# Eight experts on one core: x of the first two experts loaded into 64 rows instead of 128, b1 on another queue, the first weight load cut in two

## The chip, the core and the metric

The kernel runs on one core of a Trainium2 chip. The metric is the device time of one execution in microseconds (us); the time shown is the median of several executions. A core has TensorE (PE; its weight loads are listed apart as PEld), VectorE (DVE), ScalarE (ACT), GpSimd (POOL) and SyncE (SP). Sixteen DMA engines move data between the device memory (HBM) and the on-chip memory (SBUF, 128 rows called partitions). Programs hand transfers to them from SP, ACT or POOL.

## What is computed

Eight experts, each a two-layer network over its own 256 tokens: 512 inputs, 2048 hidden units, 512 outputs, all tensors fp32 in memory.

```python
h = np.matmul(x, w1) + b1[:, np.newaxis, :]     # x (8, 256, 512), w1 (8, 512, 2048)
h = np.maximum(h, 0)
return (np.matmul(h, w2) + b2[:, np.newaxis, :]).astype(np.float32)   # w2 (8, 2048, 512)
```

The weights are 8 x 2 x 4 MB = 67.1 MB of fp32, x and the output 4.2 MB each. Every weight is used once per token block, so the whole of it has to come in once.

## The kernel before

**Data.** w1 and w2 of an expert are loaded by POOL (`load_w1`, L82; `load_w2`, L88) and turned from fp32 into fp16 on the way, so 4 MB are read and 2 MB written, 16 KB in each of the 128 rows. POOL's transfers stand in one queue (q0 in the profile) in the order in which they are issued. x of experts 2 and 3, and of 4 to 7, comes the same way (`load_x`, L72). x of experts 0 and 1 is different: SP loads it as fp32 (L190), each expert as 128 rows of 4 KB (two tokens to a row), into two buffers of the output's pool, and DVE casts it (L201). SP's and ACT's transfers stand in queues of their own (q1 and q10).

**Stages.** `first_product(e)` (L114) makes the hidden layer of an expert: 16 column blocks `j`, each of 4 matmuls (L121) into one of three PSUM tiles, which ACT then takes through bias and Relu into `hT` (L128). It needs x transposed (`xT`), which `transposes(e)` (L95) makes on DVE in blocks of 32x32; for expert 0 it is called at the start, for expert e+1 in the middle of `first_product(e)`. A call issues 16 instructions of 256 elements a row where an x row holds two tokens (L109) or four (L112), and 8 of 512 elements where a row holds eight (L112; experts 4 to 7 before the change). `second_product(e)` (L166) runs three stages later (LAG = 3): bias b2 as a matmul with a row of ones (L171), 32 matmuls (L178), and the results through DVE and ACT (L156, L157) to the output. Results of experts 0 to 3 and 4 to 5 are held and written together by `flush` (L138) behind all weights in POOL's queue; those of 6 and 7 leave at once by SP and ACT (L164).

**Order.** PE's and POOL's instructions keep the order of the program (`ordered`); on DVE and ACT a scheduler decides. The list `ring` (L215 to L225) says in which stage each load is issued. w1 and w2 have three buffers each, so a load waits until the product that used its buffer three experts earlier is over. At the start POOL issues w1 of expert 0 (L84), b2 (L192), b1 (L196), w1 of expert 1, x of experts 2 and 3 (L76) and w1 of expert 2, before its first wait.

**b1.** b1 comes as 32 rows of 2 KB (`b_rows`) and DVE transposes it with four instructions into `b1T` (L208), which the first Relu needs.

Of the kernel before, what the change touches and what calls it, by code (L numbers as in the profile page):

```python
# [10 lines left out]
def kernel(  # L11
# [9 lines left out]
    nc = tc.nc  # L21
    fp32 = mybir.dt.float32
    fp16 = mybir.dt.float16
    E, T, H = x.shape
    M = w1.shape[2]
    P = 128
    nTB = T // P
    nKC = H // P
    nJ = M // P
    B = 32  # L30
    nB = P // B
# [9 lines left out]
    nXF32 = 2  # L41
    X_LOADS = {2: 2, 4: 4}

    def ordered(ins):
        return tc.keep_in_program_order(ins)
# [3 lines left out]
    w2_pool = ctx.enter_context(tc.tile_pool(name="w2", bufs=3))  # L49
    x_pool = ctx.enter_context(tc.tile_pool(name="xp", bufs=1))  # L50
# [3 lines left out]
    out_pool = ctx.enter_context(tc.tile_pool(name="outp", bufs=2))  # L54
# [5 lines left out]
    b1_rows = singles.tile([E * nB, M // nB], fp32)  # L60
    b1T = singles.tile([P, nJ * B + nB - 1], fp32)

    x16 = [None] * E
    xT = [None] * E
    w1_sb = [None] * E
# [15 lines left out]

    def load_w1(e):  # L82
        w1_sb[e] = w1_pool.tile([P, nKC, M], fp16, tag="w1", name="w1sb")
        ordered(nc.gpsimd.dma_start(  # L84
            out=w1_sb[e], in_=w1[e].rearrange("(p kc) m -> p kc m", kc=nKC)
        ))

    def load_w2(e):  # L88
        src = w2[e].rearrange("(p j) h -> p j h", j=nJ)
# [5 lines left out]
    def transposes(e):  # L95


        t, p0, R = x16[e]
        n = R // nTB
        xT[e] = xT_pool.tile([P, nKC, T], fp16, tag="xT", name="xT")  # L100
        for g in range(T // R // B):
            src = t[p0 + B * g : p0 + B * (g + 1)]
            for b in range(nB):
                block = src[:, :, b * (H // nB) : (b + 1) * (H // nB)].rearrange(
                    "p (n tb) (i kc) -> p tb kc n i", tb=nTB, kc=nKC)
                out = xT[e][b * B : (b + 1) * B].rearrange(
                    "p kc (tb g i n) -> p tb g kc n i", tb=nTB, i=B, n=n)
                if n == 1:
                    nc.vector.transpose(out=out[:, :, g, :, 0, :], in_=block[:, :, :, 0, :])  # L109
                    continue  # L110
                for tb in range(nTB):
                    nc.vector.transpose(out=out[:, tb, g], in_=block[:, tb])  # L112
# [71 lines left out]
                    ))  # L184
        store(e, po)

    x32 = []
    for e in range(nXF32):
        x32.append(out_pool.tile([P, nTB, H], fp32, tag="out", name="x32"))
        nc.sync.dma_start(out=x32[e], in_=x[e].rearrange("(p tb) h -> p tb h", tb=nTB))  # L190
    load_w1(0)
    ordered(nc.gpsimd.dma_start(  # L192
        out=b2_sb,
        in_=b2.rearrange("e h -> (e h)").rearrange("(o f) -> o f", o=1),
    ))
    ordered(nc.gpsimd.dma_start(out=b1_rows, in_=b1.rearrange("e (b i) -> (e b) i", b=nB)))  # L196
    nc.vector.memset(ones1, 1.0)  # L197

    for e in range(nXF32):
        t = x_pool.tile([P, nTB, H], fp16, tag=f"x{e}", name=f"x{e}")  # L200
        nc.vector.tensor_copy(out=t, in_=x32[e])  # L201
        x16[e] = (t, 0, nTB)
        if e == 0:
            transposes(e)


    for b in range(nB):
        nc.vector.transpose(  # L208
            out=b1T[b * B : (b + 1) * B, nB - 1 - b : nB - 1 - b + nJ * B],
            in_=b1_rows.rearrange("r (i j) -> r j i", j=nJ),  # L210
# [5 lines left out]
    for s in range(1, E + LAG - 1):  # L216
        if s < E:
            if s in X_LOADS:
                ring.append((s - 2, load_x, (s, X_LOADS[s])))
            ring.append((s - 2, load_w1, (s,)))  # L220
        if s >= LAG:
            ring.append((s - 2, load_w2, (s - LAG,)))
# [43 lines left out]
```

## Time and profile before

| | |
|---|---|
| median of 3 runs | 181.69 us (181.45 to 182.16) |
| profiled execution, first to last instruction (span) | 179.7 us |
| PE busy / DVE busy / ACT busy | 129.1 / 88.0 / 70.2 us |
| read from HBM / written to HBM | 71.39 MB / 4.19 MB |
| DMA queue of POOL (q0) | 38.35 MB, 96.6% of the 16 engines' span |
| DMA queue of SP (q1) / of ACT (q10) | 1.70 MB, 2.4% / 0.39 MB, 0.5% |

The times of runs are device times of a whole execution; the profile knows the span of the profiled one, and no other total of it. The span is 2.0 us below the median, and that difference lies outside the first and last instruction. A queue's megabytes are bytes written (a cast load reads twice as many). A queue's share is the time of its packets over 16 engines times the span; packets on one engine may overlap a little, so sums near or above 100% mean that the engines never stop.

### The profile page before, as it was taken

What the parts mean: (1) busy time and instruction counts of PE and PEld (TensorE: products, weight loads), DVE (VectorE), ACT (ScalarE), POOL (GpSimd) and SP (SyncE); (2) the same over time, 40 slices, a digit from 0 to 9 for tenths busy, and PEclk for the clock granted to TensorE, in tenths of its full rate; (3) what the DMA queues carried; (4) which work ended last, traced back from release to release, by engine and by line L of the source; (5) the groups of instructions that cost most, each with busy time, mean ns of one, the idle gap of its engine ahead of it and who ended that gap; (6) DMA issues with size and microseconds to landing.
All of it is one profiled execution on the core that took longest, in us unless ns stands there. A gap on an engine that the chain in (4) does not pass through costs nothing.

```text
span 179.7 us, 1958 instructions
## 1 busy us (share of the span) xinstructions
PE 129.1 (72%) x784; PEld 85.8 (48%) x784; DVE 88.0 (49%) x125; ACT 70.2 (39%) x151; POOL 13.1 (7%) x28
## 2 busy tenths in 40 slices
PE   0005099969595970899969597969497887999950
PEld 0004079969592320795369244844195332433420
DVE  0999942987000199999999998003200020301010
ACT  0000459969593022483099005950586020020010
POOL 7000002120201010001010001000200021010000
PEclk9999999999998798589999889999999996999996
DMA  5999999999999999999999999999999999999996
GB/s 216 251 226 199 233 212 197 233 224 193 228 230 192 221 233 215 197 230 230 204 208 230 219 193 233 226 193 222 230 215 197 233 206 204 223 212 215 335 420 250
DMA packets 3829, 40.56 MB, mean 226 GB/s; under 512 B 461, under 2 KB 477, under 8 KB 1133
## 3 DMA queue, kind: packets, MB, share of 16 engines
q0 software_dynamic: 3232, 38.35, 96.6%
q1 hardware_dynamic: 476, 1.70, 2.4%
q10 hardware_dynamic: 112, 0.39, 0.5%
q8 instruction: 6, 0.10, 0.2%
q14 instruction: 3, 0.02, 0.0%
HBM read 71.39 MB, written 4.19 MB: 421 GB/s over the span
## 4 chain that ended last, share of the span: by engine, by line
DMA 66%; PE 26%; POOL 2%; another core or an unknown queue 1%; issue 1%; ACT 0%; POOLq 0%
DMA w1sb<-in_w_dram 44%; DMA w2sb<-in_w_dram 22%; PE po L178 18%; PE ph L121 8%; PE po L171 1%; POOL w1sb L84 1%; ACT out L157 0%; POOL x L76 0%; POOL b_sb L192 0%; POOL b_rows L196 0%; POOLq L250 0%
## 5 line engine op out<-in xcount | busy, mean ns | idle before, releaser
L121 PE MATMUL ph<-xT,w1sb 128*128 128x256 f16 x512 | 63.6, 289 | 34.8 <-DMA w1sb<-in_w_dram 23.9
L121 PEld LDWEIGHTS <-w1sb 128*128 128x128 f16 x512 | 59.0, 147 | 40.3 <-DMA w1sb<-in_w_dram 32.6
L178 PE MATMUL po<-w2sb,hT 128*128 128x512 f16 x256 | 61.4, 402 | 9.4 <-DMA w2sb<-in_w_dram 9.4
L112 DVE STREAM_TRANSPOSE xT<-x 32x256 f16<-32x256 f16 (+1 forms) x64 | 53.1, 889 | 25.6 <-DMA x<-in_x_dram 18.7
L128 ACT ACTIVATE hT<-ph,b1T 128x256 f16<-128x256 f32 x128 | 56.2, 474 | 13.6 <-PE ph L121 13.4
L178 PEld LDWEIGHTS <-hT 128*128 128x128 f16 x256 | 25.9, 102 | 44.7 <-issue 19.3
L156 DVE COPY out<-po 32x512 f32<-32x512 f32 (+2 forms) x22 | 15.1, 688 | 54.0 <-PE po L178 53.8
L157 ACT COPY out<-po 32x512 f32<-32x512 f32 (+2 forms) x22 | 12.7, 579 | 69.7 <-PE po L178 69.5
L109 DVE STREAM_TRANSPOSE xT<-x 32x256 f16<-32x256 f16 x32 | 14.0, 436 | 0.5
L93 POOL DMA_DIRECT2D w2sb<-in_w_dram x10 | 5.3, 534 | 72.8 <-PE po L178 72.8
L128 ACT ACT_TABLE_LOAD x1 | 1.3, 1283 | 20.5 <-DVE b1T L208 20.5
L84 POOL DMA_DIRECT2D w1sb<-in_w_dram x8 | 4.5, 558 | 63.2 <-PE ph L121 62.4
L171 PE MATMUL po<-b_sb,ones 1*128 1x512 f16 x16 | 4.8, 379 | 0.0
L208 DVE STREAM_TRANSPOSE b1T<-b_rows 32x512 f32<-32x512 f32 x4 | 4.1, 1035 | 0.1
L201 DVE CAST x<-x 128x1024 f16<-128x1024 f32 x2 | 1.5, 757 | 3.3 <-DMA x<-in_x_dram 3.3
L140 POOL DMA_DIRECT2D out_dram<-out x2 | 1.1, 542 | 10.9 <-ACT out L157 10.9
L171 PEld LDWEIGHTS <-ones 1*128 1x128 f16 x16 | 0.9, 92 | 2.1 <-issue 2.1
L76 POOL DMA_DIRECT2D x<-in_x_dram x2 | 1.1, 552 | 0.0
L197 DVE MEMSET ones<- 1x128 f16 x1 | 0.2, 165 | 0.8 <-PEq L250 0.8
L196 POOL DMA_DIRECT2D b_rows<-in_b_dram x1 | 0.5, 515 | 0.0
L192 POOL DMA_DIRECT2D b_sb<-in_b_dram x1 | 0.5, 513 | 0.0
L250 POOL MEMSET const-float32-0.0<- 128x1 f32 x1 | 0.1, 99 | 0.2 <-issue 0.2
(3 smaller groups left out, 0.3 us busy)
## 6 DMA issues: line engine op xcount, KB each, us to landing
w1sb<-in_w_dram POOLq DMA_DIRECT2D x8, 2048.0 KB, 34.5
w2sb<-in_w_dram POOLq DMA_DIRECT2D x6, 2048.0 KB, 46.8
w2sb<-in_w_dram POOLq DMA_DIRECT2D x4, 1024.0 KB, 24.0
out_dram<-out POOLq DMA_DIRECT2D x1, 2048.0 KB, 26.8
x<-in_x_dram SPq DMA_DIRECT2D x2, 512.0 KB, 3.9
x<-in_x_dram POOLq DMA_DIRECT2D x1, 1024.0 KB, 30.8
out_dram<-out POOLq DMA_DIRECT2D x1, 1024.0 KB, 17.8
x<-in_x_dram POOLq DMA_DIRECT2D x1, 512.0 KB, 24.0
```

Source lines behind the costliest of these rows:

```text
L84: ordered(nc.gpsimd.dma_start(out=w1_sb[e], in_=w1[e].rearrange("(p kc) m -> p kc m", kc=nKC)))
L93: ordered(nc.gpsimd.dma_start(out=w2_sb[e][:, lo : lo + half], in_=src[:, lo : lo + half]))
L109: nc.vector.transpose(out=out[:, :, g, :, 0, :], in_=block[:, :, :, 0, :])
L112: nc.vector.transpose(out=out[:, tb, g], in_=block[:, tb])
L121: ordered(nc.tensor.matmul(out=ph, lhsT=w1_sb[e][:, kc, :].rearrange("p (q j) -> p q j", j=nJ)[:, :, j], rhs=xT[e][:, kc, :], start=(kc == 0),
L128: nc.scalar.activation(out=hT[e][:, j, :].rearrange("p (tb k i) -> p tb k i", tb=nTB, k=split), in_=ph.rearrange("p (tb i k) -> p tb k i", ...
L156: nc.vector.tensor_copy(out=out_sb[at : at + rows, k * nTB, :], in_=po[0][part])
L157: nc.scalar.copy(out=out_sb[at : at + rows, k * nTB + 1, :], in_=po[1][part])
L171: ordered(nc.tensor.matmul(out=t, lhsT=ones1, rhs=b2_sb[0:1, e * H : (e + 1) * H], start=True, stop=False,))
L178: ordered(nc.tensor.matmul(out=po[tb], lhsT=hT[e][:, j, tb * P : (tb + 1) * P], rhs=w2_sb[e][:, j, :], start=False, stop=(j == nJ - 1),))
L201: nc.vector.tensor_copy(out=t, in_=x32[e])
L208: nc.vector.transpose(out=b1T[b * B : (b + 1) * B, nB - 1 - b : nB - 1 - b + nJ * B], in_=b1_rows.rearrange("r (i j) -> r j i", j=nJ),)
```

## The change

x of experts 0 and 1 is loaded by SP as 32 rows of 16 KB for each expert (eight tokens to a row): expert 0 into rows 0 to 31, expert 1 into rows 32 to 63 of one tile. The tile is taken from w2's pool, where it fills one of three buffers. Its cast to fp16 goes into one tile `x01` and is divided: for expert 0 half on DVE and half on ACT, for expert 1 all on ACT. With eight tokens to a row, `transposes` takes the form of 8 instructions of 512 elements for both experts. The b1 load moves from POOL's queue to ACT's, as ACT's first instruction. The first w1 load becomes two transfers, rows 0 to 31 and rows 32 to 127; expert 0's matmuls wait for both. On DVE the four transposes of b1 now stand first, ahead of expert 0's cast and transposes; ACT's table load and two copies of x stand ahead of the first Relu.

```diff
     def load_w1(e):
         w1_sb[e] = w1_pool.tile([P, nKC, M], fp16, tag="w1", name="w1sb")
-        ordered(nc.gpsimd.dma_start(
-            out=w1_sb[e], in_=w1[e].rearrange("(p kc) m -> p kc m", kc=nKC)
-        ))
+        src = w1[e].rearrange("(p kc) m -> p kc m", kc=nKC)
+        rows = P // 4 if e == 0 else P
+        for lo in ((0, rows) if e == 0 else (0,)):
+            hi = rows if e == 0 and lo == 0 else P
+            ordered(nc.gpsimd.dma_start(out=w1_sb[e][lo:hi], in_=src[lo:hi]))
...
-    x32 = []
+    RX = T // B
+    x32 = w2_pool.tile([nXF32 * B, RX, H], fp32, tag="w2", name="x32")
     for e in range(nXF32):
-        x32.append(out_pool.tile([P, nTB, H], fp32, tag="out", name="x32"))
-        nc.sync.dma_start(out=x32[e], in_=x[e].rearrange("(p tb) h -> p tb h", tb=nTB))
+        nc.sync.dma_start(out=x32[e * B : (e + 1) * B], in_=x[e].rearrange("(p r) h -> p r h", r=RX))
+    nc.scalar.dma_start(out=b1_rows, in_=b1.rearrange("e (b i) -> (e b) i", b=nB))
     load_w1(0)
...
-    ordered(nc.gpsimd.dma_start(out=b1_rows, in_=b1.rearrange("e (b i) -> (e b) i", b=nB)))
     nc.vector.memset(ones1, 1.0)
 
+    x01 = x_pool.tile([nXF32 * B, RX, H], fp16, tag="x01", name="x01")
     for e in range(nXF32):
-        t = x_pool.tile([P, nTB, H], fp16, tag=f"x{e}", name=f"x{e}")
-        nc.vector.tensor_copy(out=t, in_=x32[e])
-        x16[e] = (t, 0, nTB)
+        rows = slice(e * B, (e + 1) * B)
+        cut = RX // 2 if e == 0 else 0
+        if cut:
+            nc.vector.tensor_copy(out=x01[rows, :cut], in_=x32[rows, :cut])
+        nc.scalar.copy(out=x01[rows, cut:], in_=x32[rows, cut:])
+        x16[e] = (x01, e * B, RX)
         if e == 0:
             transposes(e)
```

## The prediction, made before the changed kernel was run

> **What bounds the kernel.** I read the DMA lines of the page first, because section 2 shows them full in all slices but the first and last.
>
> ```profile
> DMA  5999999999999999999999999999999999999996
> ...
> q0 software_dynamic: 3232, 38.35, 96.6%
> q1 hardware_dynamic: 476, 1.70, 2.4%
> q10 hardware_dynamic: 112, 0.39, 0.5%
> ```
>
> The three shares add up to 99.5% of the span on all 16 engines. The chain of waits says the same in order of time: loads, then a short piece of PE work that lets the next load be issued, then loads.
>
> ```profile
> 4.00 34.57 DMA w1sb<-in_w_dram
> ...
> 46.12 45.24 DMA w1sb<-in_w_dram
> ...
> 110.12 39.38 DMA w2sb<-in_w_dram
> 149.50 0.04 issue
> 149.54 8.66 PE po L178 x32
> ```
>
> After 149.5 the chain runs on PE, which looks like a PE-bound tail. The busy time by windows corrects that (columns: window, length, busy time and count for PE, PEld, DVE, ACT, POOL, then granted clock, DMA share, GB/s):
>
> ```profile
> 0.00:1.70 1.70, 0.00 (x0) 0.00 (x0) 0.17 (x1) 0.00 (x0) 0.66 (x5) 1.00 0.00 0
> 1.70:2.30 0.60, 0.00 (x0) 0.00 (x0) 0.00 (x0) 0.00 (x0) 0.60 (x2) 1.00 0.49 137
> 2.30:4.50 2.20, 0.00 (x0) 0.00 (x0) 0.24 (x1) 0.00 (x0) 2.20 (x5) 1.00 1.03 408
> ...
> 140.00:166.00 26.00, 23.91 (x102) 9.80 (x100) 3.44 (x5) 2.54 (x5) 2.13 (x4) 0.93 1.01 212
> ...
> 168.20:178.40 10.20, 5.09 (x24) 2.12 (x22) 0.69 (x1) 0.59 (x1) 0.00 (x0) 0.92 0.94 395
> 178.40:179.70 1.30, 0.00 (x0) 0.00 (x0) 0.00 (x0) 0.00 (x0) 0.00 (x0) 0.50 0.00 0
> ```
>
> The engines start at 1.7, stop at 178.4, and have a share near 1 in between, in the tail too, where the held results fill what PE leaves open. So the span is 1.7 us before the first packet, the engines' total work, and 1.3 us after it. Only what changes that work, its start or its gaps counts; PE, DVE and ACT count only where they make a transfer late.
>
> **The change, part by part.** First the x loads, the one part that alters the engines' work. The DMA view of two windows, 0 to 5 us and 5 to 14 us:
>
> ```profile
> q1 hardware_dynamic: 287, 1.05, 54.7%
> ```
>
> ```profile
> q0 software_dynamic: 113, 1.85, 96.6%
> ```
>
> x takes 0.547 x 5.0 = 2.73 us of all 16 engines, in 256 packets of 4 KB: 2.73 x 16 / 256 = 0.171 us each. On each engine POOL's first weight packet begins within some 10 ns of the end of x there (packet records, 4.59 to 5.12 us), so the two queues together leave no hole; a change in x's time moves every later packet by the same amount. After the change x is 64 packets of 16 KB, four to an engine, all into rows 0 to 63. No row of the trace shows that, so I bound it.
>
> Low end: the held results leave in 16 KB packets of 0.611 us (packet records, 168 to 173 us), so x would cost 64 x 0.611 / 16 = 2.44 us, 0.29 us less than now. High end: the 16 KB packets that go into SBUF take 0.966 x 9.0 x 16 / 113 = 1.23 us (second fence), so x would cost 64 x 1.23 / 16 = 4.92 us, 2.19 us more. I take the high end: it is the row with the same size and the same direction, and nothing in this trace shows 16 engines filling 64 rows or fewer at full rate for longer than b1's 64 KB. Against it: those packets read 32 KB each for the cast, which plain x does not, and b1's own 32 rows came at 0.172 us per 4 KB, beside 0.159 for x's commonest packet. So both ends stay in the range.
>
> [...]
>
> The w1 load in two: the same 128 packets of 16 KB in all, one more completion packet on each engine (0.022 us in the packet records). POOL issues one w1 piece more and b1 no longer, so w1 of expert 1 is still issued near 2.9 and of expert 2 near 4.0 us (an issue took 0.5 to 0.67 us). Nobody waits: the first w1 load keeps the engines busy until 14.4. The fp16 pieces arrive at half the byte rate of plain loads, so I add nothing for rows 0 to 31 being filled alone. Cost bounds from no gain to 0.02 us; if the short first piece let weights run beside x while the engines ramp up (share 0.49 in the window 1.70 to 2.30), the gain is at most 0.51 x 0.6 = 0.3 us. I take 0.
>
> b1 on ACT: the same 64 KB, 0.17 us on each engine in either queue, so 0. ACT's issue costs it some 0.4 us (0.38 for its store at L164) before 1.3 us of table load, and nothing is queued behind these two that could run earlier.
>
> Copies of x on ACT: 512 fp32 elements took 0.58 us (L157), so 2048 and 4096 cost at most 2.3 and 4.6 us. Behind them stand the Relus, which wait for PE anyway. With x landed by about 7.1 they end before 14.5; PE has nothing for ACT before that. Cost 0.
>
> DVE, the part that gets heavier:
>
> ```profile
> L112 DVE STREAM_TRANSPOSE xT<-x 32x512 f16<-32x512 f16 x32 | 40.2, 1331 | 19.2 <-DMA x<-in_x_dram 18.7 <-PE ph L121 0.3
> ...
> L109 DVE STREAM_TRANSPOSE xT<-x 32x256 f16<-32x256 f16 x32 | 14.0, 436 | 0.5
> ```
>
> An expert's transposes go from 16 x 0.436 = 7.0 us to 8 x 1.331 = 10.6 us, the same form that experts 4 to 7 use. b1 now stands ahead. It comes behind x on the engines, so it lands near 7.3 us; four transposes of 1.035 us (L208) end at 11.4, the half cast of 2048 elements (twice 0.757) at 12.9, xT of expert 0 at 23.5 us. Before, PE had 12 matmuls done and stood still from 18.05 to 22.28, because ACT waited for b1T. From 22.28 on it needed 8.2 us to the end of the product (POOL's next w1 issue at 30.46). Now: 23.5 + 2.8 (the 12 matmuls) + 8.2 = 34.5 us. POOL's w1 load of expert 3 waits for that. The engines have work until w1 of expert 2 is in, 36.8 us by the first engines before and about 39.0 with x longer: 4.5 us of cover, 2.3 without the longer x (then b1 and the product are 2 us earlier as well). Expert 1's xT is ready at 34.1, in time; its product ends near 41.5 and expert 2's starts then, 0.8 us behind its weights, and waits again for expert 3's weights (47.66 before). So the heavier DVE work is hidden. If the cover were gone, each further microsecond would cost one.
>
> The tile in w2's pool: w2 of expert 2 now waits for the release of x32, over before 15 us; it was issued at 46.65. Cost 0.
>
> Sum: 2.19 us on the span, 179.7 to 181.9; the 2.0 us around it stay, so the median goes from 181.69 to **183.9 us** (+1.2%).
>
> **The rivals.** *The rows do not matter* (no change). x's packets cost 0.153 to 0.171 us per 4 KB wherever they land: between -0.29 and 0, so 181.4 to 181.7 us. For it: b1's 32 rows at 0.172, and 96 rows stored by ACT at 0.159 without any spread; against it: the first lasted under a microsecond, the second reads SBUF and alternates with other packets. A change that did not do what it says (16 KB rows cut again into 4 KB packets) would end here too.
>
> *The start is filled* (faster). Weights in the short first piece run beside x from its first packet: 0.29 from cheaper packets and 0.3 from the ramp give 181.1 us. It decides only if more than 0.91 us comes together, which is 0.3 us more than the rows hold; that could come from the last engine, since w1 of expert 2 landed on 15 engines by 37.14 and on the last at 38.57. I know no reason why x in new rows should cure that.
>
> *The DVE order starves POOL* (slower). If xT of expert 0 comes later than 23.5 by more than the 4.5 us of cover, for example because b1 lands behind much of w1, the queue runs dry; b1 landing at 14 would give 23.5 + 6.7 = 30.2, 2.2 us over the cover, so 183.9 + 2.2 = 186.1 us.
>
> **How the numbers follow.** About 0.5%, 0.91 us, is what a measurement of this kernel can tell from no change. Rows matter, with all or half of the high end: 0.68, its own range 183.0 to 184.4. Rows do not matter: 0.22. Start filled past 0.91 us: 0.06. POOL starved: 0.04. Slower 0.68 + 0.04 = 0.72, same 0.22, faster 0.06. The range reaches from 181.1, which takes in the second case with its gain, to 184.4; it leaves out the last two and the edges.
>
> **What would show it.** Right: q1's 64 packets of 16 KB near 1.2 us each, POOL's first weight packet near 6.9 us instead of 4.6, w1 of expert 0 landing near 17.4 instead of 15.2, every later landing 2 us late, and DMA shares near 1 throughout. Wrong: x packets near 0.61 us, or a DMA share well below 1 between 30 and 45 us (then DVE starved the queue).

## The result and the profile after

The changed kernel takes **183.78 us** (median of 4 runs, 183.63 to 183.88); the kernel before, on the same chip, 181.62 us (181.45 to 182.16). The ratio is 1.011, with a 95% interval of 1.0095 to 1.0125. Forecast were 183.9 us and a range of 181.1 to 184.4. The span grew from 179.7 to 182.0 us, 2.3 us, so the whole difference lies between the first and the last instruction.

The page's DMA lines show queues as full as before, and SP's queue with 284 packets instead of 476, yet 3.4% of the engines' time instead of 2.4%:

```profile
DMA  6999999999999999999999999999999999999995
...
q0 software_dynamic: 3216, 38.28, 95.2%
q1 hardware_dynamic: 284, 1.70, 3.4%
q10 hardware_dynamic: 160, 0.46, 0.7%
```

The bytes in q1 are the same 1.70 MB. One percent more of 182 us is 1.8 us: x has become dear. Its part alone, in the DMA view of 0 to 9 us (packets, MB, share of 16 engines):

```profile
q1 hardware_dynamic: 96, 1.05, 51.2%
q0 software_dynamic: 32, 0.52, 29.1%
q10 hardware_dynamic: 48, 0.07, 3.6%
```

That is 0.512 x 9.0 = 4.61 us for x, where it was 2.73, and 0.036 x 9.0 = 0.32 us for b1. In the packet records the 64 packets of x take 1.273 us in the median, the first of each engine 0.63 to 1.10, the rest up to 1.30. POOL's first weight packet of an engine starts at 7.02 us on average, at 4.77 before: 2.25 us later. From there on, up to 166 us, the engines stay as full as before (columns as in the prediction; a row counts a packet's whole time where the packet starts, so a short window can show more than 1):

```profile
1.70:2.30 0.60, 0.00 (x0) 0.00 (x0) 0.00 (x0) 0.60 (x1) 0.60 (x2) 1.00 1.10 328
2.30:6.70 4.40, 0.00 (x0) 0.00 (x0) 0.60 (x1) 1.08 (x2) 2.23 (x5) 1.00 0.98 212
6.70:30.00 23.30, 8.57 (x60) 7.77 (x61) 23.00 (x20) 10.62 (x16) 0.00 (x0) 1.00 1.02 213
30.00:38.00 8.00, 6.89 (x64) 6.68 (x63) 7.87 (x18) 6.73 (x16) 1.59 (x3) 1.00 1.07 229
38.00:46.00 8.00, 6.78 (x63) 6.55 (x62) 6.51 (x17) 6.60 (x16) 1.06 (x2) 1.00 1.00 213
46.00:166.00 120.00, 96.18 (x562) 60.88 (x561) 53.75 (x52) 48.53 (x105) 6.89 (x13) 0.91 1.02 216
```

The second row is the loss in one line: the engines are as busy as before (0.98), but move 212 GB/s, in a stretch where x moved at 408 before (window 2.30 to 4.50). The fence has no hole between 30 and 46 us (shares 1.07 and 1.00), where a late DVE leaves one in the run with 12.4 us more below (0.26).

The chain of waits now begins differently, on DVE:

```profile
0.73 5.34 DMA b_rows<-in_b_dram
...
29.76 0.51 issue
30.27 1.34 DVE xT L114
31.61 0.14 issue
31.74 7.20 PE ph L123 x64
...
47.65 45.71 DMA w1sb<-in_w_dram
```

Read alone, it would blame b1 and the transposes, 16% of the span between them. It does not know that the loads which PE's work releases at 39 us join a queue that is still full (share 1.00 from 38 to 46 us); two experiments below show that this stretch costs nothing.

### The profile page after: what moved, and what is told of

Read it like the earlier page. It is cut to its first block, busy times and chain, and to the rows that moved or that the text cites. A ratio compares the mean times of both kernels' runs of the same rounds, so it can differ in the third digit from the quotient of the medians.

```text
span 182.0 us, 1945 instructions
## 1 busy us (share of the span) xinstructions
PE 128.2 (70%) x784; PEld 85.8 (47%) x784; DVE 93.3 (51%) x108; ACT 75.8 (42%) x153; POOL 13.0 (7%) x28
## 4 chain that ended last, share of the span: by engine, by line
DMA 50%; PE 26%; DVE 14%; issue 5%; another core or an unknown queue 1%; POOL 1%; ACT 0%; DVEq 0%; POOLq 0%
DMA w1sb<-in_w_dram 25%; DMA w2sb<-in_w_dram 22%; PE po L180 17%; DVE xT L114 11%; PE ph L123 8%; DMA b_rows<-in_b_dram 3%; DVE b1T L214 2%; PE po L173 1%; DVE x L206 1%; ACT out L159 0%; POOL w1sb L88 0%; POOL w2sb L95 0%; DVEq L114 0%; POOLq L95 0%
## 5 line engine op out<-in xcount | busy, mean ns | idle before, releaser
L114 DVE STREAM_TRANSPOSE xT<-x 32x512 f16<-32x512 f16 (+1 forms) x80 | 72.7, 977 | 21.1 <-DMA x<-in_x_dram 19.0
L180 PE MATMUL po<-w2sb,hT 128*128 128x512 f16 x256 | 59.9, 395 | 8.0 <-DMA w2sb<-in_w_dram 8.0
L207 ACT CAST x<-x 32x2048 f16<-32x2048 f32 (+1 forms) x2 | 5.5, 2750 | 4.0 <-DMA x<-in_x_dram 4.0
L206 DVE CAST x<-x 32x2048 f16<-32x2048 f32 x1 | 1.2, 1214 | 0.0
```

What stands on the lines that cost most here:

```text
L180: ordered(nc.tensor.matmul(out=po[tb], lhsT=hT[e][:, j, tb * P : (tb + 1) * P], rhs=w2_sb[e][:, j, :], start=False, stop=(j == nJ - 1),))
L206: nc.vector.tensor_copy(out=x01[rows, :cut], in_=x32[rows, :cut])
L207: nc.scalar.copy(out=x01[rows, cut:], in_=x32[rows, cut:])
```

## The experiments

Theory: the place of x, rows 0 to 63, makes its packets slow (1.273 us in the median) and so keeps the DMA engines busy longer, and the rest follows one for one; the expectations call it the theory of place. Rivals: packet size, the other parts of the change, the DVE order.

**x as before, the rest kept.**

```diff
-    x32 = w2_pool.tile([nXF32 * B, RX, H], fp32, tag="w2", name="x32")
+    x32.append(out_pool.tile([P, nTB, H], fp32, tag="out", name="x32"))      # for e in 0, 1
-        nc.sync.dma_start(out=x32[e * B : (e + 1) * B], in_=x[e].rearrange("(p r) h -> p r h", r=RX))
+        nc.sync.dma_start(out=x32[e], in_=x[e].rearrange("(p tb) h -> p tb h", tb=nTB))
...
```

> The changed kernel with x of experts 0 and 1 loaded and cast as before (128 rows of 4 KB); b1 on ACT's queue and the first w1 load in two stay. Theory (the x load alone costs the time): x's packets 0.16 us again, POOL's first weight packet near 4.8 us, 181.3 to 181.9 us. Rival (the split of w1 or b1 beside x costs part of it): 182.5 us or more.

Measured: 181.77 us, 1.0005 times the kernel before (0.9996 to 1.0014). x took 2.79 us of the engines. The first weight packet of an engine came at 5.22 us on average, not near 4.8: b1's packets, 0.41 us in this run, now stand ahead of it instead of behind it. Without x in 64 rows there is no loss to measure.

**x alone.** The kernel before with the changed load, cast and transposes of x, b1 and w1 as they were.

> The kernel before with x of experts 0 and 1 as 32 rows of 16 KB each, and nothing else of the change. Theory (the x load alone costs the time): x's packets near 1.27 us, first weight packet near 7.0 us, 183.4 to 184.2 us. Rival (the other parts cost): under 182.6 us.

Measured: 183.25 us, 1.0083 (1.007 to 1.0097), a little below the range expected; packets 1.274 us, first weight packet at 6.70 us on average. x makes 1.6 of the 2.2 us by itself. In the DMA view of 0 to 9 us its packets take 53.4%, 4.81 us, which is 2.07 more than before: the time follows the packets here only to about 0.4 us. The 0.5 us missing appear only with the other parts beside it, and two experiments further down look for them.

**The same packets, other rows.** One transfer of 64 rows of 16 KB into rows 32 to 95, 0 to 63, or 64 to 127:

```diff
-    x32 = w2_pool.tile([nXF32 * B, RX, H], fp32, tag="w2", name="x32")
-    for e in range(nXF32):
-        nc.sync.dma_start(out=x32[e * B : (e + 1) * B], in_=x[e].rearrange("(p r) h -> p r h", r=RX))
+    AT = 32        # 0 and 64 in the other two
+    x32 = w2_pool.tile([P, RX, H], fp32, tag="w2", name="x32")
+    nc.sync.dma_start(out=x32[AT : AT + nXF32 * B], in_=x[0:nXF32].rearrange("e (p r) h -> (e p) r h", r=RX))
...                # the casts use the same rows of x01
```

Rows 32 to 95:

> The changed kernel with x of both experts in one transfer of 64 rows of 16 KB into rows 32 to 95 instead of 0 to 63; same packets, same DVE work. [...] Rival of size (a 16 KB packet, or fewer rows than 128, is slow in itself): packets 1.27 us, 183.4 to 184.0 us.

Rows 0 to 63:

> As the kernel with rows 32 to 95, but the one transfer of 64 rows goes into rows 0 to 63. Theory of place: packets 1.2 to 1.3 us, 183.4 to 184.2 us. Rival (two transfers of 32 rows one after the other were the trouble, and one of 64 cures it): packets 0.61 us, near 181.4 us.

Rows 64 to 127:

> As the kernel with one transfer of 64 rows, into rows 64 to 127. [...] Rival (the low rows alone are crowded, by something else that lives or writes there): packets 0.61 us, 181.7 to 182.1 us.

Measured:

| rows | time, us | ratio to before | packet of x, median |
|---|---|---|---|
| 32 to 95 | 181.96 | 1.0015 (1.0006 to 1.0024) | 0.618 us |
| 0 to 63 | 183.66 | 1.0104 (1.0089 to 1.0120) | 1.287 us |
| 64 to 127 | 183.32 | 1.0088 (1.0069 to 1.0107) | 1.280 us |

In the DMA view of 0 to 9 us, rows 32 to 95 first, then rows 0 to 63, then rows 64 to 127:

```profile
q1 hardware_dynamic: 80, 1.05, 31.8%
```

```profile
q1 hardware_dynamic: 80, 1.05, 51.1%
```

```profile
q1 hardware_dynamic: 80, 1.05, 52.6%
```

Packets, bytes, instructions on DVE and their order are the same in the three; the engines' time for x is 2.86, 4.60 and 4.73 us. Only the place of the rows differs. That excludes size and number of rows as the cause of the slow packets, and the third excludes that the low rows alone are crowded: either half is slow (1.287 and 1.280 us), and half of each is fast (0.618). What lies behind this is not shown. The first gains nothing over the kernel before: even with 16 KB packets of 0.618 us x costs 2.86 us, where it was 2.73, because the first packet of an engine takes up to 1.58 us and starts at 2.10 us at the earliest, behind b1 (1.74 us in the changed kernel).

**Packets of 4 KB into the same rows.** Each expert's x in four transfers of 4 KB to a row.

```diff
-        nc.sync.dma_start(out=x32[e * B : (e + 1) * B], in_=x[e].rearrange("(p r) h -> p r h", r=RX))
+        src = x[e].rearrange("(p r) h -> p r h", r=RX)
+        for r in range(0, RX, 2):
+            nc.sync.dma_start(out=x32[e * B : (e + 1) * B, r : r + 2], in_=src[:, r : r + 2])
```

> The changed kernel with each expert's 32 rows of 16 KB fetched in four transfers of 4 KB to a row, into the same rows 0 to 63. Theory of place: 4 KB packets near 0.32 us instead of 0.16, x 4.6 to 5.0 us of the engines, 183.6 to 184.2 us. Rival of size (16 KB packets are slow): packets 0.16 us, 181.6 to 182.0 us.

Measured: 184.26 us, 1.0137 (1.0119 to 1.0156). The time fits the theory, most of the packets do not: their median is 0.172 us. SP needed 5.0 us to issue the eight transfers, POOL's weights began at 2.97 us, and x came in single packets between them until 24 us. Why most were short is not shown. In a stretch where many of x's packets ran together, 2.75 to 3.03 us, 12 of 15 took 0.27 to 0.34 us, the doubled time that the theory asks for. The first weight packets took 1.24 to 2.08 us. Expert 0's x was late as well, and w1 of expert 3 was issued only at 36.23 us. This run mixes several effects. Of its 2.7 us, 1.35 are longer packet times of all queues together; the rest, engines that stand idle in the first 8 us and at the end, stays open.

**Half the amount.** Expert 0's x in 32 rows, expert 1's in 128.

```diff
+    x32 = w2_pool.tile([B, RX, H], fp32, tag="w2", name="x32")
+    nc.sync.dma_start(out=x32, in_=x[0].rearrange("(p r) h -> p r h", r=RX))
+    x32b = out_pool.tile([P, nTB, H], fp32, tag="out", name="x32b")
+    nc.sync.dma_start(out=x32b, in_=x[1].rearrange("(p tb) h -> p tb h", tb=nTB))
...
```

> The changed kernel with expert 0's x alone in 32 rows of 16 KB; expert 1's comes in 128 rows of 4 KB. Theory of place: expert 0's packets 1.2 us, expert 1's 0.16, half the loss: 182.5 to 183.0 us. Rival (a fixed cost of this form of load, whatever its amount): 183.6 us or more, or 181.8 or less.

Measured: 182.62 us, 1.0049 (1.0032 to 1.0066): 1.05 us over the 181.57 of the kernel before, half of the whole change's 2.16. Expert 0's packets took 1.06 us in the median (1.2 expected), expert 1's 0.169.

**DVE's order.** The four transposes of b1 two times and four times, ahead of (or among) expert 0's transposes:

```diff
-    for b in range(nB):
+    for b in [b for _ in range(2) for b in range(nB)]:        # 4 in the second
         nc.vector.transpose(out=b1T[...], in_=...)
```

> The changed kernel with the four transposes of b1 done twice, 4.1 us more on DVE ahead of expert 0's x. Theory (DVE's heavier start is hidden by loads already issued): POOL issues w1 of expert 3 near 35 us instead of 30.9, before the engines run out near 38.9; 183.6 to 184.0 us, no change from the changed kernel. Rival (DVE's order is part of the loss): 185 us or more.

> The changed kernel with the transposes of b1 done four times, 12.4 us more on DVE. Theory: the cover is gone; w1 of expert 3 is issued near 43.3 us, the engines stand idle from 38.9 to some 44.5 us, and the end comes later by that, 188.5 to 190.5 us. Rival (DVE's start never matters): 183.8 us.

Measured: 183.66 us with 4.1 us more, as the changed kernel (183.78). With 12.4 us more the runs spread from 187.5 to 190.3 us, median 189.63, and why they spread is open. The profiled execution, 190.32 us, is the slowest of them, and the ratio, 1.0389 (1.0324 to 1.0454), leaves it out. POOL issued w1 of expert 3 at 35.04 and 42.99 us (30.93 in the changed kernel). The windows of 30 to 46 us, first with 4.1, then with 12.4 us more:

```profile
30.00:38.00 8.00, 6.84 (x63) 6.63 (x62) 7.91 (x11) 6.68 (x16) 1.59 (x3) 1.00 1.06 227
38.00:46.00 8.00, 8.00 (x76) 8.00 (x75) 7.05 (x19) 8.00 (x19) 1.06 (x2) 1.00 0.99 212
```

```profile
30.00:38.00 8.00, 6.28 (x29) 4.78 (x29) 7.86 (x8) 2.63 (x6) 0.00 (x0) 1.00 1.07 229
38.00:46.00 8.00, 6.54 (x54) 6.03 (x52) 7.91 (x10) 5.65 (x13) 1.59 (x3) 1.00 0.26 33
```

The DMA share falls to 0.26 only in the last row: 0.74 x 8 = 5.9 us without transfers. By the packet records the engines run dry between 38.6 and 39.2 us, and the next packets begin at 44.25. The median grew by 5.85 us, the span of the profiled execution by 6.5. So the changed kernel's DVE work lies wholly under loads already issued, with more than 4.1 us to spare.

**The other two parts, beside x in rows 0 to 63.** First the w1 load whole again, then b1 back on POOL's queue:

```diff
-        for lo in ((0, rows) if e == 0 else (0,)):
-            ...
+        ordered(nc.gpsimd.dma_start(out=w1_sb[e], in_=w1[e].rearrange("(p kc) m -> p kc m", kc=nKC)))
```

> The changed kernel with the first w1 load whole again; x in rows 0 to 63 and b1 on ACT's queue stay. The kernel with x alone took 183.25 us, the whole change 183.78 us. If the first piece of w1 (its packets 1.28 and 1.33 us instead of 1.23, all into rows 0 to 31) makes up part of those 0.5 us: first two weight packets of an engine at 1.23 us, 183.5 to 183.7 us. Rival (the split costs nothing, b1 all): 183.8 us.

```diff
-    nc.scalar.dma_start(out=b1_rows, in_=b1.rearrange("e (b i) -> (e b) i", b=nB))
+    ordered(nc.gpsimd.dma_start(out=b1_rows, in_=b1.rearrange("e (b i) -> (e b) i", b=nB)))   # behind b2
```

> The changed kernel with b1 back on POOL's queue behind b2; x in rows 0 to 63 and w1 in two stay. If b1 beside x makes up part of the 0.5 us (its packets took 0.32 us of the engines there, 0.17 on POOL's queue): 183.4 to 183.6 us. Rival (the split of w1 is all): 183.8 us.

Measured: 183.53 (183.45 to 183.62) and 183.50 us (183.47 to 183.61), each about 0.25 below the changed kernel's 183.78 (183.63 to 183.88). Together that is about the 0.5 us that x alone left open. But by their ratios to the kernel before, 1.0101 (1.0085 to 1.0116) and 1.0101 (1.0086 to 1.0116), neither can be told from the changed kernel's 1.011 (1.0095 to 1.0125), so what each part costs is not shown. Without the split an engine's first two weight packets take 1.29 and 1.23 us, with it 1.29 and 1.33.

**A version with what is good in the change.** x of both experts in one transfer of 128 rows of 8 KB, b1 on ACT's queue, w1 whole; DVE casts expert 0's half, ACT expert 1's.

```diff
+    RX = nXF32 * T // P
+    x32 = w2_pool.tile([P, RX, H], fp32, tag="w2", name="x32")
+    nc.sync.dma_start(out=x32, in_=x[0:nXF32].rearrange("e (p r) h -> (e p) r h", r=RX))
...
```

> A version meant to keep what is good: x of both experts in one transfer of 128 rows of 8 KB, cast half on DVE and half on ACT, b1 on ACT's queue, the first w1 load whole. Theory (the engines' total work sets the time): x 2.5 to 2.7 us of the engines, 181.4 to 181.9 us, no measurable gain although ACT no longer waits for b1. Rival (the wait for b1T at the start costs time): 180.7 us or less.

Measured: 181.75 us, 1.0007 (0.9998 to 1.0017). It issues w1 of expert 3 at 26.35 us instead of 30.46, four microseconds earlier, and gains nothing. No version here beats the kernel before.

## Why the prediction was right, step by step

**The bound.** That only the engines' work, start and gaps count was right, in both directions: PE's stall for b1T removed (x as before; 128 rows of 8 KB) bought nothing, and 4.1 us more on DVE cost nothing. The packet times of all queues, added up over the profile and divided by 16 engines, are 179.3 us before. They are 2.0 us more with the change, 2.1 and 1.9 with one transfer into rows 0 to 63 and 64 to 127, 1.8 with x alone, 1.0 with half the amount, and no more with rows 32 to 95; the times grew by 2.16, 2.04, 1.75, 1.63, 1.05 and 0.34 us. So one for one holds to about 0.35 us. The run with 4 KB packets is the exception (1.35 and 2.7).

**The x load.** The step chosen between two bounds, 1.23 us for a 16 KB packet rather than 0.61, was right: 1.273 in the median. The reason given with it, the same size and direction as the weights' packets, was not: into rows 32 to 95 packets of this size and direction took 0.618 us, and only the place of the rows differs there. That the place matters was shown by no row of the trace before; the three placements show it. Here x was in flight from 1.74 to 7.36 us, 187 GB/s by 1.05 MB over 5.6 us. The measured size of the term was 4.61 us, not 4.92, because the first packet of each engine took only 0.63 to 1.10 us: +1.88 instead of +2.19.

**Two terms priced at nothing** were not quite nothing. In the changed kernel's packet records b1 took 0.32 us of the engines instead of 0.17, and an engine's second weight packet 1.33 us instead of 1.23. With x's 1.88 this makes 2.13 of the 2.16 us. The runs that take back one part came out 0.25 us (the split) and 0.28 us (b1) faster, which is not clear of noise, and the packets do not explain it: with b1 back on POOL's queue x's packets took 4.87 us instead of 4.61, so x and b1 together took no less. The price of each part stays open, somewhere between 0.1 and 0.3 us. With x in 128 rows the two together were within the measurement, although b1 took 0.41 us there. That 183.9 came so near to 183.78 is in part luck: x was put 0.31 us too high, and these two terms about as much too low.

**DVE.** The direction was right, the size was not: xT of expert 0 was ready at 21.43 us, not 23.5. b1 landed at 6.07, not 7.3, since its packets went between those of x (2.81 to 4.79 us, x until 7.36) instead of behind them; the cast took 1.21 us, not 1.5, and the eight transposes 9.8, not 10.6. From there to POOL's issue at 30.93 it took 9.5 us, not 11.0 (2.8 + 8.2). Both of these terms held a slow start of PE after standing still: in the kernel before 12 matmuls took 2.77 us after 15.28 us without one (64 took 7.21 later), and after another 4.22 us the Relus followed each other at 0.85 us instead of 0.44. The changed kernel has such a start only once in this product, after 21.43 us (Relus at 0.85 us from 22.48 to 25.04, then 12 in 5.28). By the prediction's reckoning the cover was then 38.9 - 30.93 = 8.0 us rather than 4.5. That reckoning leaves out the time from an issue to its first packet, 1.3 us in the run with 12.4 us more (42.99 to 44.25). There the issue came 12.06 us later than in the changed kernel and the engines stood idle for 5.6 us by the packet records, so some 6.4 us were covered.

**The rivals.** *The rows do not matter* is refuted by the placements. *The start is filled* did not happen: no weight packet started before 6.70 us, and by the packet records the engines were in use for 0.43 of the window 1.70 to 2.30, as before (0.44). *DVE starves POOL* has the right mechanism, as 12.4 us more show, and does not set in here.

## What to carry to other kernels

Where the DMA engines never stop, price a change first by the engines' time for its packets (here good to some 0.35 us); a chain of waits that runs over other engines can be covered by transfers already queued (here 4.1 us more on DVE cost nothing, 12.4 us more cost 5.85), and the DMA share by windows tells whether it is (1.06 and 0.99 against 1.07 and 0.26). Where a load fills only part of the rows, measure it at more than one place: here a 16 KB packet took 0.618 us into rows 32 to 95, 1.28 to 1.29 into rows 0 to 63 or 64 to 127. Larger packets bought nothing here: packets of 4 and 8 KB into 128 rows and of 16 KB into rows 32 to 95 cost 2.79, 3.01 and 2.86 us for the same 1.05 MB.

## What the runs showed that was not expected

- Where x was issued in one or two transfers, all of it went ahead of the weights. In the kernel before, the engines' first weight packets started from 4.59 us on, each within some 10 ns of an end of x; in the changed kernel so from 6.70 us on. With x issued in eight pieces over 5.0 us they started from 2.97 us on, and x then waited among the weights until 24 us. What sets this order is not shown.
- The first piece of w1 fills 32 rows alone. Where x had just gone into rows 0 to 63, an engine's second weight packet took 1.31 to 1.33 us instead of 1.23. With the same piece behind x in 128 rows, in rows 32 to 95 or in rows 64 to 127 it took 1.23. So 32 rows alone do not slow a cast load here, and why they do behind x in rows 0 to 63 stays open.
